# A transformer trunk on one core: first two projections interleaved, gate columns moved into the value weights, and the first query copies kept in the value tile

## The chip, the cores and the metric

The kernel runs on one core of a Trainium2 chip. The metric is the device time of one execution in microseconds (us). Three executions of the kernel before took 1258.33, 1259.99 and 1260.75 us.

## The reference

A trunk of two layers over 512 tokens of width 1024, with a memory of 256 rows that each layer attends to. Layer 0 mixes tokens by gated linear attention (GLA), layer 1 by a sparse attention (NSA); each layer ends in an FFN with a short convolution. The change touches layer 0 up to its memory attention:

```
xn = rmsnorm(h, norm_mix[i])
mem_kv = rmsnorm(mem, norm_mem[i]) @ w_mem_kv[i]
q, k, v, g, lr, mq = split_cols(xn @ gla_w_in[i], GLA_SIZES)   # 384, 384, 768, 768, 16, 256
log_a = log_sigmoid(lr @ gla_w_gate_up[i] + gla_b_gate[i]) / GLA_GATE_NORM
main = gla_mixer(q, k, v, log_a, g, gla_out_norm[i])
mo = mem_attention(mq, mem_kv)           # 4 heads of 64, softmax over 256 memory rows
h = h + concat([main, mo]) @ w_out[i]
h = h + conv_ffn(rmsnorm(h, norm_ffn[i]), ...)
```

## The kernel before, in words

Activations lie transposed: `h[k]` is a tile of 128 features by 512 tokens, k from 0 to 7. All large products run on TensorE (PE) as three fp32r matmuls on a split of each operand in a high part (`xh`, `wh`, a rounded copy made by ScalarE, ACT) and a low part (`xl`, `wl`, the remainder, made by VectorE, DVE): `xh·wh`, `xh·wl`, `xl·wh`. So one projection of 128 columns over 8 tiles of h is 24 matmuls of 512 columns (`projA`), and a projection whose result lies by tokens (`stepsB`, values) is, for each k and each of the four 128-token tiles, 3 matmuls. The rms norm's gain is folded into the split of h, and its row factor is applied later: `rms_sums` (sums of squares by 16 one-column matmuls, then the power on GpSimd, POOL) and `rms_rows` (four transposes, copied to `rb`).

Weights are packed in chunks of 128x1024 (512 KB). `wget` loads one by a DMA on SyncE's (SP's) queue into a `wraw` buffer (3 of them), and splits it into a `wh` and a `wl` buffer (3 each); so a split waits for the PE to be done with the chunk three before, and a load for the split of the chunk three before.

PSUM has four pairs of banks, `acc`, `sc`, `pt`, `po`. The framework orders the instructions of each engine by a planner with costs; `behind(a, b)` only forces a after b on an engine and adds no wait of its own.

The order of layer 0 before, on the PE: ten idle matmuls on ones; `glak[0]`, row by row as `h` comes in (L525), with the gate's small projection `lr` in three pieces between (L530: plain fp32, 16 output columns, summed from three places of a bank); `glaq[0]` and `glak[1]`, the latter with `rms_sums` and `rms_rows` in it; `glaq[1]`; the decays' up-projection `z` (L605) into two `po` and two `pt` banks, followed on ACT and DVE by Abs, Exp, Ln and a combining step (L606 to L611) that reads `z` again, and by the copies `lad` (`spread`, L615); `glak[2]` and `glaq[2]`; the memory's keys (`memk0`, two chunks, into `acc`) and values (`memv0`, into `po`); the memory queries (`glamq`, two chunks); then the memory attention, with the 768 value columns as filler between its steps (`fill`): 512 columns in four chunks, 256 in two.

For the memory attention the key and query halves of each head are stacked on 128 partitions: `dup` copies 64 rows twice by DMA (`kd` or `mt` from `mkf`, `qd` from `sq`), and the parts (`stack_k`, `stack_q`) are made from the copy. The keys' copies are issued by SP, those of the first queries by ACT's own queue. In the kernel before the query copies lie in tiles of the pool `mema0`.

Of the kernel before, what the change touches and what calls it, by code (L numbers as in the profile page):

```python
# [48 lines left out]
def pack_weights(i):  # L49
# [22 lines left out]
    moving("glav", gw, ar(1280, 1536), 4)  # L72
# [82 lines left out]
def host_inputs(i):  # L155
# [8 lines left out]
        "wlr": np.ascontiguousarray(_blocks(gw, np.arange(2304, 2320), 16)),  # L164
# [11 lines left out]
class Trunk:  # L176
# [29 lines left out]
    def setup(self):  # L206
        nc, I = self.nc, self.I
        self.wlr = self.const.tile([128, 152], F32, tag="wlr", name="wlr")[:, 24:]
        self.vec = self.t(self.const, [128, V_N], "vec")
        self.gains = self.t(self.const, [128, 64], "gains")  # L210
        self.h = [self.t(self.keep, [128, S], f"h{k}") for k in range(KC)]
        row = lambda eng, k: eng.dma_start(self.h[k], I["xT"][128 * k:128 * k + 128, :])
        self.raw = self.t(self.wraw, [128, 1024], "wraw")
        part = lambda c: nc.sync.dma_start(self.raw[:, 512 * c:512 * c + 512], I["wp"][self.W["glak"][0]][:, 512 * c:512 * c + 512])
# [12 lines left out]
        idle = self.ps("pt")  # L227
        for _ in range(10):
            nc.tensor.matmul(idle[:, :128], self.ones, self.ones, start=True, stop=True)
        self.mhalf = self.t(self.const, [128, 8], "mhalf")  # L230
        nc.scalar.activation(self.mhalf, self.ones[:, :8], AF.Copy, scale=-0.5)
# [5 lines left out]
    def gain(self, n, k):  # L237
        return self.gains[:, 8 * n + k:8 * n + k + 1]


    def wload(self, i):
        raw = self.t(self.wraw, [128, 1024], "wraw")
        self.nc.sync.dma_start(raw, self.I["wp"][i])
        return raw

    def wget(self, i, gain=None, ks=range(KC)):

        nc = self.nc
        raw = self.wload(i)
        wh = self.t(self.wsp, [128, 1024], "wh", FR)  # L250
        wl = self.t(self.wsp, [128, 1024], "wl", FR)
# [6 lines left out]
        if gain is not None:  # L258
            a, n = 8 * gain + ks[0], len(ks)
            g = self.gains[:, a:a + n].unsqueeze(2).to_broadcast([128, n, 1024 // n])  # L260
# [26 lines left out]
    def projA(self, ps, w, M=128, N=S, x=None, late=False, at=()):  # L287


# [6 lines left out]
        for n, (k, u, i) in enumerate(steps):  # L296
            if n in at:
                at[n]()
            self.last = self.nc.tensor.matmul(ps[:M, :N], u[:, M * k:M * k + M], x[k][i][:, :N], start=n == 0, stop=n == 23)  # L299

# [4 lines left out]
    def stepsB(self, name, first, rows, N, banks, x, gain=None):  # L305

        nc = self.nc
        for c in range(KC // rows):
            ks = range(rows * c, rows * c + rows)
            wh, wl = self.wget(self.W[name][first + c], gain, ks)  # L310
# [30 lines left out]
    def rms_sums(self, N, tag):  # L341
# [7 lines left out]
        self.powed = nc.gpsimd.tensor_tensor(out=self.rc, in0=self.rc, in1=self.mhalf[:, :nt], op=ALU.pow)  # L349

    def rms_rows(self, N, tag, after=None):

        pb = self.ps("pt")
# [23 lines left out]
    def stack_k(self, dst, kd):  # L377

        nc = self.nc
        nc.scalar.activation(dst, kd, AF.Copy)  # L380
        return nc.vector.tensor_tensor(out=dst[64:], in0=kd[64:], in1=dst[64:].bitcast(F32), op=ALU.subtract)

    def stack_q(self, qf, pool, qpool, bufs=1, eng=None):

        out = []
        for hh in range(2):
            qd = self.t(qpool, [128, S], "qd", bufs=2)
# [15 lines left out]
    def mem_kv(self, l, keep):  # L403
        nc, I = self.nc, self.I
        mK = []
        with self.tc.tile_pool(name=f"memp{l}", bufs=2, side="right") as pool:
# [10 lines left out]
            pk = [self.ps("acc") for _ in range(2)]  # L417
            self.projA(pk[0], self.wget(self.W[f"memk{l}"][0]), N=MEM, x=mx, at={12: lambda: self.rms_sums(MEM, "m")})
            self.projA(pk[1], self.wget(self.W[f"memk{l}"][1]), N=MEM, x=mx)
# [11 lines left out]
            for m in range(2):  # L431
                for hh in range(2):
# [3 lines left out]
                    self.stack_k(K, kd)  # L436
# [7 lines left out]
    def mem_att(self, qfs, pool, mK, mV, mo, first, fill, qpool, eng=None):  # L444
# [48 lines left out]
        Q[0] = self.stack_q(qfs[0], pool, qpool, eng=eng)  # L493
        first()
        for i in range(10):
            if i < 8:
                scores(*divmod(i, 4))
            if i == 3:
                Q[1] = self.stack_q(qfs[1], pool, qpool)
# [7 lines left out]
    def gla_layer(self):  # L507
        nc, I, tc = self.nc, self.I, self.tc
        with ExitStack() as outer:
# [8 lines left out]
            with tc.tile_pool(name="glap", bufs=1) as pp:  # L518
                wlr = self.wlr.rearrange("p (k c) -> p k c", k=8)
                nc.gpsimd.tensor_tensor(out=wlr, in0=wlr, in1=self.gains[:, :8].unsqueeze(2).to_broadcast([128, 8, 16]), op=ALU.mult)  # L520
                ps = self.ps("po")
                qps = [self.ps(tag) for tag in ("acc", "acc", "sc")]
                wh = self.t(self.wsp, [128, 1024], "wh", FR)
                wl = self.t(self.wsp, [128, 1024], "wl", FR)
                first = lambda u, k, i, **kw: nc.tensor.matmul(qps[0], u[:, 128 * k:128 * k + 128], self.x[k][i], **kw)  # L525

                def small(a, b, after):
                    for n in range(a, b):
                        o = 32 * ((n + 1) % 3)
                        gate = nc.tensor.matmul(ps[o:o + 16], wlr[:, n], self.h[n], start=n < 3, stop=n >= 5)  # L530
                        self.behind(gate, after)
                    return gate

                for k in range(KC):
                    self.split_x(0, [k])
                    if k < 2:
                        c = slice(512 * k, 512 * k + 512)
                        self.split_to(wh[:, c], wl[:, c], self.raw[:, c])
                    gate = small(0, 2, last) if k == 1 else None
                    for i in range(2):  # L540
                        last = first(wh, k, i, start=k + i == 0, stop=False)
                        if gate is not None:
                            self.behind(last, gate)
                    if k >= 2:
                        first(wl, k - 2, 0, start=False, stop=False)
                    if k == 4:
                        small(2, 5, last)
                for k in (KC - 2, KC - 1):
                    last = first(wl, k, 0, start=False, stop=k == KC - 1)
                small(5, 8, last)  # L550
                early = []
                for r, (name, j) in enumerate((("glaq", 0), ("glak", 1))):
                    for k in range(3 * r, 3 * r + 1 + 2 * r):
                        self.sq_step(k, self.h[k], S, after=self.made)
                    early.append(self.wget(self.W[name][j]))
                    if not r:
                        for k in (1, 2):
                            self.sq_step(k, self.h[k], S, after=self.made)
                nc.sync.dma_start(self.vec, I["vec"])
                for k in range(6, KC):  # L560
                    self.sq_step(k, self.h[k], S, after=self.made)

                def queries_keys(i):
# [3 lines left out]
                    else:  # L567
                        qp = self.ps("sc" if i == 3 else "acc")
                        self.projA(qp, self.wget(self.W[("glak", "glaq")[r]][j]))
                    sc = DK ** -0.5 if r else 1.0  # L570
                    for lo, hi, dst in ((0, DK, qk[:, :, r, j, :]), (DK, 128, qk[32 * j:32 * j + 32, :, r, 3, :])):
                        nc.vector.scalar_tensor_tensor(out=dst, in0=qp[lo:hi].rearrange("p (c t) -> p c t", c=4), scalar=sc,
                                                       in1=rb[lo:hi].rearrange("p (c t) -> p c t", c=4), op0=ALU.mult, op1=ALU.mult)

                for i in (1, 2):
                    self.projA(qps[i], early[i - 1], late=i == 1, at=self.rms_at(6, 18) if i == 2 else ())
                rc, rb = self.rc, self.rb
# [10 lines left out]
                lr = self.t(pp, [128, S], "lr")  # L588
                nc.gpsimd.memset(lr, 1.0)
                nc.scalar.copy(lr[:16], ps[:16])  # L590
                nc.vector.tensor_tensor(out=lr[:16], in0=ps[32:48], in1=lr[:16], op=ALU.add)
                nc.vector.tensor_tensor(out=lr[:16], in0=ps[64:80], in1=lr[:16], op=ALU.add)
                lrs = self.t(self.tmp, [128, S], "sq", FR, bufs=2)
                nc.vector.tensor_tensor(out=lr[:16], in0=lr[:16], in1=rb[:16], op=ALU.mult)
                nc.scalar.activation(lrs[:64], lr[:64], AF.Copy)
                nc.vector.tensor_tensor(out=lrs[64:], in0=lr[:64], in1=lrs[:64].bitcast(F32), op=ALU.subtract)
                for i in range(4):
                    queries_keys(i)
# [3 lines left out]
                for c in range(4):  # L602
                    z = self.ps("pt" if c >= 2 else "po")
                    for i, g in enumerate(gus):
                        nc.tensor.matmul(z[:, :384], lrs[:97, 128 * c:128 * c + 128], g, start=i == 0, stop=i == 1)  # L605
                    nc.scalar.activation(la[:, c, :], z[:, :384], AF.Abs)  # L606
                    pz.append(z)
                nc.scalar.activation(la, la, AF.Exp, scale=-1.0)
# [9 lines left out]
                for i in (4, 5):  # L618
                    queries_keys(i)
# [7 lines left out]
                with tc.tile_pool(name="memk0", bufs=1, side="right") as mk:  # L627
                    mK, mV = self.mem_kv(0, mk)
                    with tc.tile_pool(name="mema0", bufs=1, side="right") as mp:
# [3 lines left out]
                        for m in range(2):  # L633
                            qfs.append(self.project_q(w, rb, self.tmp, bufs=2, tag="sq"))
                            if m == 0:
                                w = self.wget(self.W["glamq"][1])

                        def values():
                            for g, (rows, N) in enumerate(((2, 512), (4, 256))):
# [883 lines left out]
```

## Time and profile before

| | |
|---|---|
| times of three runs | 1258.33, 1259.99, 1260.75 us; median 1259.99 |
| profiled execution | 1260.37 us, of which the span from first to last instruction is 1258.6 us |
| granted TensorE clock | 0.999 |
| PE, DVE, ACT, POOL busy | 1248.6, 816.4, 605.5, 119.0 us |
| chain that ended last | PE 91%, DMA 3%, DVE 3%, ACT 2% |

A row of the profile has the engine, the line of the kernel, the operation, the tile written and those read, shapes and a count. A matmul's own duration overlaps the next one; what a matmul costs in a stream is the distance from its start to the next start. In the timeline the bracket gives how long an engine was idle before the row and what released it.

### The profile page before, as it was taken

What the parts mean: (1) busy time and instruction counts of PE and PEld (TensorE: products, weight loads), DVE (VectorE), ACT (ScalarE), POOL (GpSimd) and SP (SyncE); (2) the same over time, 40 slices, a digit from 0 to 9 for tenths busy, and PEclk for the clock granted to TensorE, in tenths of its full rate; (3) what the DMA queues carried; (4) which work ended last, traced back from release to release, by engine and by line L of the source; (5) the groups of instructions that cost most, each with busy time, mean ns of one, the idle gap of its engine ahead of it and who ended that gap; (6) DMA issues with size and microseconds to landing.
All of it is one profiled execution on the core that took longest, in us unless ns stands there. A gap on an engine that the chain in (4) does not pass through costs nothing.

```text
span 1258.6 us, 18412 instructions
## 1 busy us (share of the span) xinstructions
PE 1248.6 (99%) x7054; PEld 1043.6 (83%) x7054; DVE 816.4 (65%) x1380; ACT 605.5 (48%) x1136; POOL 119.0 (9%) x144
## 2 busy tenths in 40 slices
PE   9999999999999999999999999999999999999998
PEld 6888889888888888888888788888888888888887
DVE  7756886577777774334677877855777777773331
ACT  7546654454444443223455677763544444442231
POOL 1000000000000000000102366650000000000000
PEclk9999999999999999999999999999999999999999
DMA  7651112343333333333766432303233333333321
GB/s 246 159 164 62 34 42 77 93 119 94 92 99 101 101 90 95 101 101 93 211 177 183 128 112 79 104 10 99 85 101 101 95 92 99 101 105 89 95 84 68
DMA packets 44891, 131.53 MB, mean 105 GB/s; under 512 B 6036, under 2 KB 11702, under 8 KB 44804
## 3 DMA queue, kind: packets, MB, share of 16 engines
q1 hardware_dynamic: 43124, 128.64, 35.3%
q10 hardware_dynamic: 1680, 1.72, 0.5%
q8 instruction: 56, 0.92, 0.3%
q14 instruction: 31, 0.25, 0.1%
HBM read 116.13 MB, written 2.15 MB: 94 GB/s over the span
## 4 chain that ended last, share of the span: by engine, by line
PE 91%; DMA 3%; DVE 3%; ACT 2%; issue 1%; SPq 0%; ACTq 0%; POOL 0%; POOLq 0%; DVEq 0%
PE acc L299 41%; PE acc L958 17%; PE acc L894 6%; PE po L1256 3%; PE acc L680 3%; PE acc L1256 3%; PE sc L1256 2%; PE pt L1257 2%; PE acc L1027 2%; PE acc L1170 2%; PE po L317 2%; PE sc L894 1%; DMA wraw<-in_wp 1%; PE pt L746 1%; PE acc L317 1%
## 5 line engine op out<-in xcount | busy, mean ns | idle before, releaser
L264 DVE TENSOR_TENSOR wl<-wraw,wh 128x1024 fp32r<-128x1024 f32 x180 | 229.3, 1274 | 139.8 <-ACT wh L263 137.3
L299 PE MATMUL acc<-xh,wh 128*128 128x512 f32 x792 | 308.9, 390 | 0.0
L299 PE MATMUL acc<-xl,wh 128*128 128x512 f32 x792 | 308.2, 389 | 0.0
L299 PE MATMUL acc<-xh,wl 128*128 128x512 f32 x792 | 307.0, 389 | 0.0
L263 ACT ACTIVATE wh<-wraw 128x1024 fp32r<-128x1024 f32 x180 | 190.8, 1060 | 226.7 <-PE acc L958 75.0
L299 PEld LDWEIGHTS acc<-xh,wh 128*128 128x128 f32 x792 | 148.7, 188 | 31.6 <-ACT sq L328 0.9
L299 PEld LDWEIGHTS acc<-xl,wh 128*128 128x128 f32 x792 | 148.7, 188 | 31.0
L299 PEld LDWEIGHTS acc<-xh,wl 128*128 128x128 f32 x792 | 148.7, 188 | 30.5
L958 PE MATMUL acc<-ah,wh 128*128 128x512 f32 x308 | 119.8, 389 | 0.0
L958 PE MATMUL acc<-ah,wl 128*128 128x512 f32 x308 | 119.8, 389 | 0.0
L958 PE MATMUL acc<-al,wh 128*128 128x512 f32 x308 | 119.8, 389 | 0.0
L939 DVE TENSOR_TENSOR u<-acc,rb 128x512 f32<-128x512 f32 x88 | 60.5, 688 | 73.7 <-PE acc L299 69.1
L277 ACT ACTIVATE ah<-hc 128x512 fp32r<-128x512 f32 x44 | 27.8, 632 | 117.1 <-DVE hc L946 117.1
L941 ACT ACTIVATE hc<-u,vec 128x512 f32<-128x512 f32 x88 | 71.1, 808 | 2.7 <-DVE u L939 2.0
L943 DVE SCALAR_TENSOR_TENSOR hc<-u,vec,hc 128x510 f32<-128x510 f32 x88 | 66.0, 750 | 3.0
L958 PEld LDWEIGHTS acc<-al,wh 128*128 128x128 f32 x308 | 57.8, 188 | 12.1
L945 ACT ACTIVATE hc<-hc 128x512 f32<-128x512 f32 x44 | 27.8, 632 | 83.1 <-DVE hc L943 83.0
L958 PEld LDWEIGHTS acc<-ah,wl 128*128 128x128 f32 x308 | 57.8, 188 | 12.0
L958 PEld LDWEIGHTS acc<-ah,wh 128*128 128x128 f32 x308 | 57.8, 188 | 11.9
L942 DVE SCALAR_TENSOR_TENSOR hc<-u,vec,hc 128x511 f32<-128x511 f32 x88 | 65.5, 744 | 1.8 <-ACT hc L941 1.8
L1335 POOL TENSOR_TENSOR P<-P,ssm 128x256 f32<-128x256 f32 (+3 forms) x48 | 63.3, 1339 | 1.8
L1327 ACT ACTIVATE P<-P,smn 128x128 f32<-128x128 f32 (+3 forms) x96 | 53.3, 558 | 6.6 <-DVE smn L1325 6.0
(407 smaller groups left out, 2107.4 us busy)
## 6 DMA issues: line engine op xcount, KB each, us to landing
wraw<-in_wp SPq DMA_DIRECT2D x197, 512.0 KB, 3.6
strip<-vecd SPq DMA_DIRECT2D x12, 448.0 KB, 4.1
qd<-qf SPq DMA_DIRECT2D x24, 128.0 KB, 2.4
h<-in_xT SPq DMA_DIRECT2D x8, 256.0 KB, 5.2
mt<-in_memT SPq DMA_DIRECT2D x16, 128.0 KB, 3.5
kd<-kf SPq DMA_DIRECT2D x16, 128.0 KB, 2.4
lad<-la SPq DMA_DIRECT2D x4, 384.0 KB, 7.5
qd<-sq SPq DMA_DIRECT2D x12, 128.0 KB, 2.8
```

Source lines behind the costliest of these rows:

```text
L263: self.made = nc.scalar.activation(wh, raw, AF.Copy)
L264: self.left = nc.vector.tensor_tensor(out=wl, in0=raw, in1=wh.bitcast(F32), op=ALU.subtract)
L299: self.last = self.nc.tensor.matmul(ps[:M, :N], u[:, M * k:M * k + M], x[k][i][:, :N], start=n == 0, stop=n == 23)
L894: self.nc.tensor.matmul(ps[:, cols], a[:, o], b[:, cols], start=start and i == 0 and k == ks[0], stop=stop and k == 5 and i == 2)
L939: nc.vector.tensor_tensor(out=u, in0=ps, in1=rb, op=ALU.mult)
L941: nc.scalar.activation(c, u, AF.Identity, scale=tap(2), bias=tap(3))
L942: nc.vector.scalar_tensor_tensor(out=c[:, 1:], in0=u[:, :S - 1], scalar=tap(1), in1=c[:, 1:], op0=ALU.mult, op1=ALU.add)
L943: nc.vector.scalar_tensor_tensor(out=c[:, 2:], in0=u[:, :S - 2], scalar=tap(0), in1=c[:, 2:], op0=ALU.mult, op1=ALU.add)
L958: nc.tensor.matmul(ps, a[:, o], x, start=n == 0, stop=n == 3 * NJ - 1)
L1256: mm = lambda *args, **kw: pe(nc.tensor.matmul(*args, **kw))
L1327: nc.scalar.activation(P[:, br, :n], P[:, br, :n], AF.Exp, scale=-1.0, bias=mn[:, br:br + 1], accum_out=f[:, j, br:br + 1])
L1335: nc.gpsimd.tensor_tensor(out=P, in0=P, in1=f[:, i, :].unsqueeze(2).to_broadcast([128, 2, 128 * t + 128]), op=ALU.mult)
```

## The change

- **Opening.** The first chunk of the queries is loaded beside that of the keys, both in halves between the rows of `h`, and `glak[0]` and `glaq[0]` run interleaved, in an order written out by hand (`begin`), with the splits on ACT and DVE chained in program order (`chained`). The row gains for the first norm come as an 8x128 tile `gT`, transposed on the PE behind the fifth of now nine idle matmuls; the load of the first 64 gain columns and the tile `gains` go, and later gains are read from `vec`.
- **Gate.** The gate's 16 columns are packed behind the last 256 value columns: `glavg`, four chunks of 128x544 used, 272 moving columns. This product now runs right after `glak[1]`, into banks `po`, `po`, `sc`, `pt`, with `rms_sums` and `rms_rows` in it; its gate columns are scaled (`lrT`), transposed back by four PE transposes during `glaq[1]` (`rows`), split, and the four decay products run between the matmuls of `glaq[1]` (`decay`, at steps 13, 16, 19, 22), the third into an `acc` bank.
- **Order.** `glak[2]` and `glaq[2]` move into the filler of the memory attention, in place of the 256 value columns; the memory's keys go to `sc` banks.
- **Query copies.** The copies `qd` lie in `v[:, t, :512]`, which the value product fills only later. ACT issues the copies of the first queries ahead of the last two memory keys' high parts, and DVE scales the first queries ahead of these keys' low parts.

```
-    moving("glav", gw, ar(1280, 1536), 4)
+    both = np.concatenate([ar(1280, 1536), ar(2304, 2320)])
+    a = _blocks(gw, both, 272).reshape(128, 4, 544)
...
 def setup(self):
         row(nc.sync, 0)
-        nc.scalar.dma_start(self.gains, I["vec"][:, :64])
-        nc.scalar.dma_start(self.wlr, I["wlr"])
-        part(0)
+        nc.scalar.dma_start(gT, I["gT"])
+        part(0, 0)
         row(nc.sync, 1)
-        part(1)
-        for k in range(2, KC):
+        part(1, 0)
+        row(nc.sync, 2)
+        row(nc.sync, 3)
+        part(0, 1)
+        row(nc.sync, 4)
+        part(1, 1)
+        for k in range(5, KC):
             row(nc.sync, k)
...
+        turned = nc.tensor.transpose(idle[:, 128:136], gT, self.ident[:8, :8])
+        self.behind(turned, last)
+        nc.vector.tensor_copy(self.first, idle[:, 128:136])
...
 def mem_kv(self, l, keep, banks="acc"):
+            w = self.wget(self.W[f"memk{l}"][1])
+            if l == 0:
+                self.behind(self.made, self.rowed)
...
+                    low = self.stack_k(K, kd)
+                    if m:
+                        self.later.append((self.made, low))
...
 def mem_att(...):
+        Q[0] = self.stack_q(qfs[0], pool, lambda hh: homes(0, hh), eng=eng)
+        if eng is not None:
+            for made, low in self.later:
+                self.behind(made, self.copied)
...
 def gla_layer(self):
+                row(0)
+                halfw(0, 0)
+                begin(A(H, 0), A(L, 0))
+                row(1)
+                begin(A(H, 1), A(Wl, 0), A(Wl, 1))
+                halfw(1, 0)
+                begin(B(H, 0), B(H, 1), A(L, 1), B(L, 0), B(L, 1))
+                row(2)
+                begin(A(H, 2), B(H, 2), B(Wl, 0), B(Wl, 1), A(Wl, 2), B(Wl, 2), A(L, 2), B(L, 2))
...
+                self.projA(qps[2], third, late=True)
...
+                pv = [self.ps(tag) for tag in ("po", "po", "sc", "pt")]
+                for n, _ in enumerate(self.stepsB("glavg", 0, 2, 272, pv, self.x)):
+                    if n == 4:
+                        bank = self.rms_sums(S, "")
+                    if n == 9:
+                        self.rms_rows(S, "", self.last, bank)
...
+                def rows():
+                    pb = self.ps("po")
+                    for t in range(4):
+                        self.behind(nc.tensor.transpose(pb[:16, 128 * t:128 * t + 128], lrT[:, t], self.ident), self.last)
+                    self.rowed = nc.scalar.activation(lrs[:16], pb[:16], AF.Copy)
...
+                at = {13 + 3 * c: lambda c=c: decay(c) for c in range(4)}
+                at[4] = rows
+                for _ in queries_keys(3, None, at):
+                    pass
...
-                    mK, mV = self.mem_kv(0, mk)
+                    mK, mV = self.mem_kv(0, mk, "sc")
...
+                                for made, low in self.later:
+                                    self.behind(low, self.evacuated)
...
+                            yield from self.stepsB("glav", 0, 2, 512, pv, self.x)
+                            for t in range(4):
+                                nc.scalar.activation(v[:, t, :512], pv[t], AF.Copy, scale=rc[:, t:t + 1])
+                            for i in (4, 5):
+                                yield from queries_keys(i)
...
-                            upto(6)()
+                            upto(6 if len(calls) < 5 else 9)()
-                        self.mem_att(qfs, mp, mK, mV, mo, upto(8), fill, mp, nc.scalar)
+                        self.mem_att(qfs, mp, mK, mV, mo, upto(8), fill, lambda m, hh: v[:, 2 * m + hh, :512], nc.scalar)
```

More of the change, by code (lines that the diff above doesn't have):

```diff
@@ L227, in setup @@
         idle = self.ps("pt")
-        for _ in range(10):
-            nc.tensor.matmul(idle[:, :128], self.ones, self.ones, start=True, stop=True)
+        warm = lambda: nc.tensor.matmul(idle[:, :128], self.ones, self.ones, start=True, stop=True)
+        for _ in range(5):
+            last = warm()
+        turned = nc.tensor.transpose(idle[:, 128:136], gT, self.ident[:8, :8])
+        self.behind(turned, last)
+        nc.vector.tensor_copy(self.first, idle[:, 128:136])
+        for _ in range(4):
+            self.behind(warm(), turned)
         self.mhalf = self.t(self.const, [128, 8], "mhalf")
@@ L309, in stepsB @@
             ks = range(rows * c, rows * c + rows)
-            wh, wl = self.wget(self.W[name][first + c], gain, ks)
+            wh, wl = self.wget(self.W[name][first + c], gain, ks, rows * N)
             for r, k in enumerate(ks):
@@ L527, in small @@
[L527 to L534, printed above, removed]
-                    self.split_x(0, [k])
[L536 to L558, printed above, removed]
+                ws = [[self.t(self.wsp, [128, 1024], tag, FR) for tag in ("wh", "wl")] for _ in range(2)]
@@ new lines, in gla_layer, with chained, row, halfw @@
+                first = []
+                splits = []
+                def chained():
+                    for ins, n in ((self.made, 0), (self.left, 1)):
+                        if splits:
+                            self.behind(ins, splits[0][n])
+                    splits[:] = [(self.made, self.left)]
+                def row(k):
+                    self.split_x(0, [k])
+                    chained()
+                def halfw(n, c):
+                    c = slice(512 * c, 512 * c + 512)
+                    self.split_to(ws[n][0][:, c], ws[n][1][:, c], self.raw[n][:, c])
+                    chained()
@@ new lines, in begin @@
+                def begin(*parts):
+                    for n, u, i, k in parts:
+                        ins = nc.tensor.matmul(qps[n], ws[n][u][:, 128 * k:128 * k + 128], self.x[k][i], start=k + u + i == 0, stop=k == KC - 1 and i == 1)
+                        if first:
+                            self.behind(ins, first[0])
+                        first[:] = [ins]
+                H, L, Wl = (0, 0), (0, 1), (1, 0)
+                A, B = ((lambda p, k, n=n: (n, *p, k)) for n in range(2))
+                row(0)
@@ L559, in gla_layer @@
+                begin(A(H, 4), A(Wl, 4))
+                halfw(1, 1)
+                begin(B(H, 4), A(L, 4), B(L, 4), B(Wl, 4))
+                for k in range(5, KC):
+                    row(k)
+                    begin(*(t(p, k) for p in (H, Wl, L) for t in (A, B)))
+                self.sq_step(0, self.h[0], S, after=self.made)
+                third = self.wget(self.W["glak"][1])
                 nc.sync.dma_start(self.vec, I["vec"])
-                for k in range(6, KC):
+                for k in range(1, KC):
@@ L567, in queries_keys @@
                     else:
-                        qp = self.ps("sc" if i == 3 else "acc")
-                        self.projA(qp, self.wget(self.W[("glak", "glaq")[r]][j]))
+                        qp = self.ps("acc")
+                        yield from self.stepsA(qp, self.wget(self.W[("glak", "glaq")[r]][j]), at=steps)
                     sc = DK ** -0.5 if r else 1.0
                     for lo, hi, dst in ((0, DK, qk[:, :, r, j, :]), (DK, 128, qk[32 * j:32 * j + 32, :, r, 3, :])):
[L572 to L577, printed above, removed]
+                        ins = nc.vector.scalar_tensor_tensor(out=dst, in0=qp[lo:hi].rearrange("p (c t) -> p c t", c=4), scalar=sc,
+                                                             in1=rb[lo:hi].rearrange("p (c t) -> p c t", c=4), op0=ALU.mult, op1=ALU.mult)
+                        if after is not None:
+                            self.behind(ins, after)
+                self.projA(qps[2], third, late=True)
                 gup = self.t(pp, [128, 384], "gup")
```

120 lines of the change are left out of this document (63 added, 57 removed).

## The prediction

> **What bounds the kernel now.** I read the page first, then the PE's timeline up to 120 us, then ACT, DVE and SP around the places where the PE waits.
>
> ```profile
> PE 1248.6 (99%) x7054; PEld 1043.6 (83%) x7054; DVE 816.4 (65%) x1380; ACT 605.5 (48%) x1136; POOL 119.0 (9%) x144
> ```
>
> The PE is the bound: of the span's 1258.6 us only 10 have no matmul running. A busy PE need not be at its pace, so the pace is taken from start to start. In these rows of the PE's timeline the reader is to look at the first column; between the pairs lie 14, 34 and 4 intervals:
>
> ```profile
> 16.47 0.39 PE L299 MATMUL acc<-xl,wh 128*128 128x512 f32 x1
> 19.66 0.39 PE L299 MATMUL acc<-xl,wh 128*128 128x512 f32 x1
> 48.42 0.28 PE L299 MATMUL acc<-mh,wl 128*128 128x256 f32 x1
> 52.50 0.28 PE L299 MATMUL acc<-ml,wh 128*128 128x256 f32 x1
> 34.06 0.86 PE L605 MATMUL po<-wg,sq 97*128 97x384 f32 x4
> 34.76 0.85 PE L605 MATMUL pt<-wg,sq 97*128 97x384 f32 x4
> ```
>
> 512 columns take 3.19/14 = 0.2275 us, 256 take 4.08/34 = 0.12, 384 take 0.70/4 = 0.175. One column more costs (0.2275 - 0.12)/256 = 0.42 ns. Held against these paces, the starts up to 120 us show time lost in only three places, all touched by the change: the opening with the gate's pieces, the norm sums, and the first scores of the memory attention.
>
> **The opening, term a.** First two windows (busy time by engine; last the clock, DMA share and GB/s), then what ACT, DVE and the PE did:
>
> ```profile
> 2.00:12.00 10.00, 8.59 (x41) 5.26 (x39) 6.27 (x10) 8.00 (x13) 0.40 (x1) 1.00 1.00 362
> 5.83:21.70 15.87, 15.15 (x64) 9.04 (x65) 14.11 (x19) 13.85 (x22) 1.85 (x3) 1.00 0.93 321
> 3.85 0.72 ACT L280 ACTIVATE xh<-h,gains 128x512 fp32r<-128x512 f32 x1 [0.69 <-DMA gains<-in_vec]
> 5.14 0.63 ACT L277 ACTIVATE wh<-wraw 128x512 fp32r<-128x512 f32 x1 [0.57 <-DMA wraw<-in_wp]
> 7.17 0.63 ACT L277 ACTIVATE wh<-wraw 128x512 fp32r<-128x512 f32 x1 [0.58 <-DMA wraw<-in_wp]
> 8.61 4.13 DVE L281 SCALAR_TENSOR_TENSOR xl<-h,gains,xh 128x512 fp32r<-128x512 f32 x6
> 5.83 0.50 PE L525 MATMUL acc<-xh,wh 128*128 128x512 f32 x1 [0.69 <-ACT wh L277]
> 15.16 1.04 PE L530 MATMUL po<-h,wlr 128*16 128x512 f32 x6
> 16.13 0.50 PE L299 MATMUL acc<-xh,wh 128*128 128x512 f32 x1
> ```
>
> From 5.83 to 21.70, where the third projection starts, 64 matmuls run: 48 of two projections, worth 48 x 0.2275 = 10.92, and the gate's 16. A piece of six holds the PE for 16.13 - 15.16 = 0.97. The rest of the 15.87 is waiting for rows.
>
> After, the 16 go, and 48 matmuls have two weight halves to work on. The first needs the gain, row 0 and the first half. `gT` is an eighth of the bytes of the load it replaces, and waits for five idle matmuls; the half landed at 5.14 and keeps its place in the queue, so I leave the first matmul at 5.8. Then five matmuls can run (to 6.95) until the first half of the queries, which takes the queue place of the half that landed at 7.17, is split on ACT by 7.8. That is a stall of 0.9; 43 matmuls are left, and end at 7.8 + 43 x 0.2275 = 17.6. Is the rest in time? Twelve pieces of 0.262 MB are 3.15 MB; at 362 GB/s from 2.0 they drain by 10.7, and a piece lands up to 2 later (the one of 7.17 ends 1.15 MB into the queue, drained by 5.2 at this rate), so row 7 is there by 12.7. ACT has 8 x 0.72 + 4 x 0.63 = 8.3 us of splits from 3.9, with waits for two landings: done near 13.5. DVE has 4.13/6 = 0.69 to 0.75 a row and 0.69 a half: done near 14.3. The PE comes to row 7 at 16.2. So the third projection starts at 17.6 in place of 21.70: **a = -4.1**. With the stall gone and a start at 5.6 it is -4.7; with rows 0.9 later than the PE wants them -3.2.
>
> **Sums, columns and transposes, terms b, c, d.**
>
> ```profile
> 23.52 0.39 PE L299 MATMUL sc<-xl,wh 128*128 128x512 f32 x1
> 24.06 0.63 PE L338 MATMUL pt<-ones,sqacc 128*64 128x1 f32 x16 [0.15 <-DVE sqacc L332]
> 24.62 0.50 PE L299 MATMUL sc<-xh,wh 128*128 128x512 f32 x1
> 26.80 0.60 PE L355 MATMUL pt<-ident,rc 128*128 128x128 f32 x4
> 27.15 0.48 PE L299 MATMUL sc<-xh,wh 128*128 128x512 f32 x1
> ```
>
> The sums waited 24.06 - 23.75 = 0.3 for DVE. In the value product they come at 17.6 + 5.46 + 12 x 0.127 = 24.6, while the squares' adds can start near 15: **b = -0.3** (0 if DVE is late again). The four row transposes, 27.15 - 26.80 = 0.35, only move.
>
> The value product has 96 matmuls of 272 instead of 256 columns: 96 x 16 x 0.42 ns, **c = +0.65**; it costs 12.2 at its new place, and the keys and queries 4 and 5 give 10.9 of filler where it gave 11.5. Four chunks instead of two are 2 more splits; DVE, which was busy 14 of the opening's 16 us, is freed of the gate's adds, and the PE has three chunks ahead, so I cost them at nothing; if that cover were gone, a chunk's two splits, some 1.3 by the whole chunk's 2.3, would show.
>
> Four new transposes bring `lrT` back: **d = +0.35**, by the rows just used. They are pinned behind matmul 4 of `glaq[1]`, so every later matmul waits with them for DVE's four small scalings and for a `po` bank; the first decay is pinned 9 matmuls (2.0 us) behind, with ACT's copy and a DVE subtraction between. If DVE has one chunk's split in front, d is 1.3. The decay matmuls cost 8 x 0.175 as before.
>
> **The first queries' copies, term e.** Three views: ACT, DVE and the PE around the first scores; and the landing times of the tile `qd`.
>
> ```profile
> 64.04 0.39 PE L299 MATMUL acc<-xh,wh 128*128 128x512 f32 x1
> 64.96 0.42 ACT L380 ACTIVATE mK<-mkd 128x256 fp32r<-128x256 f32 x1 [2.27 <-DMA mkd<-mkf]
> 65.87 0.69 DVE L400 SCALAR_TENSOR_TENSOR sq<-acc,rb 128x512 f32<-128x512 f32 x1
> 66.65 2.47 ACTq L375 DMA_DIRECT2D qd<-sq  x4
> 73.22 0.63 ACT L277 ACTIVATE Qh<-qd 128x512 fp32r<-128x512 f32 x1 [6.07 <-DMA qd<-sq]
> 75.21 0.28 PE L454 MATMUL sc<-mK,Ql 128*128 128x256 f32 x1
> 75.99 0.39 PE L454 MATMUL sc<-mK,Qh 128*128 128x256 f32 x1 [0.50 <-ACT Qh L277]
> 76.72 0.39 PE L454 MATMUL sc<-mK,Ql 128*128 128x256 f32 x1 [0.34 <-DVE Ql L278]
> DMA to landing us min/median/max: 2.3/4.9/6.1
> ```
>
> The scores lose 75.99 - 75.33 and 76.72 - 76.11, 1.27 in all. The cause lies ten microseconds earlier: the scaling of the queries (65.87) stands on DVE behind the last key's low part, which needs the key's copy (64.96), while the first queries' product was through at 64.04, where the second one's stream begins. The change lifts the scaling to about 64.2 and the issue to 65.0, 1.7 earlier. The keys moved behind are needed only four scores later, some 20 us on: nothing for them. Landing then decides. The copies took up to 6.1 us, the first pair from 66.65 to 73.22; after the change the decays' copies (next) come nearer too. **e = -1.0**, between -1.27 and 0.
>
> [...]
>
> **The decays' chain, term f.** ACT, DVE, SP and the PE in order of time, a window, and from the page the splits of a weight chunk on DVE and ACT (mean ns of one behind the comma):
>
> ```profile
> 37.11 1.47 ACT L608 ACTIVATE la<-la 128x1536 f32<-128x1536 f32 x1
> 38.60 1.28 ACT L609 ACT_TABLE_LOAD   x1
> 39.89 1.58 ACT L609 ACTIVATE la<-la,ones 128x1536 f32<-128x1536 f32 x1
> 41.51 1.02 DVE L611 SCALAR_TENSOR_TENSOR la<-po,la 128x384 f32<-128x384 f32 x2 [1.76 <-ACT la L609]
> 43.52 1.37 SPq L615 DMA_DIRECT2D lad<-la  x2
> 46.35 0.28 PE L299 MATMUL acc<-mh,wh 128*128 128x256 f32 x1
> 52.62 0.28 PE L317 MATMUL po<-wh,mh 128*128 128x256 f32 x1
> 45.00:58.00 13.00, 13.00 (x109) 12.62 (x108) 8.36 (x13) 3.47 (x4) 0.70 (x1) 1.00 1.02 233
> L264 DVE TENSOR_TENSOR wl<-wraw,wh 128x1024 fp32r<-128x1024 f32 x180 | 229.3, 1274 | 139.8 <-ACT wh L263 137.3
> L263 ACT ACTIVATE wh<-wraw 128x1024 fp32r<-128x1024 f32 x180 | 190.8, 1060 | 226.7 <-PE acc L958 75.0
> ```
>
> The memory values (52.62) take the two `po` banks that hold `z` until DVE's last step (41.51). That left 10 us; the change takes nearly all of it. By my walk: third projection 17.6 to 23.1, value product with sums and rows to 36.2, `glaq[1]` with 0.35 and 1.4 to 43.4, memory keys 6.27 (52.62 - 46.35) to 49.7. The last decay ends near 43.0; Abs 0.4, Exp 1.47, table 1.28, Ln 1.58, two steps of 0.51 bring the `po` banks free at 48.8. Slack 0.9. But ACT and DVE must also split the memory values' first chunk (1.06 and 1.27), whose buffer comes free at 43.4: ahead of Exp it delays the banks to 49.9, behind Ln it comes itself at 51. **f = +0.4**, between 0 and 1.4. The copies `lad` move from 43.5 to 50 on SP, and with them the stretch from 45 to 58, in which DMA was full (share 1.02): up to the keys' copies, and towards those of the queries. Their own reader comes only in the filler, over 20 us on.
>
> **Sum.** -4.1 - 0.3 + 0.65 + 0.35 - 1.0 + 0.4 = **-4.0**. The profiled execution took 1260.37, its span 1258.6 and 1.8 around it; so 1256.4 for it, and against the median 1259.99, 0.4 lower, **1256.0**. Ends: -4.7 - 0.3 + 0.65 + 0.3 - 1.27 = -5.3, 1254.7; -3.2 + 0.65 + 1.3 + 1.4 = +0.15, 1260.1.
>
> **The rivals.**
> *The earlier copies land no earlier* (e = 0). For it: DMA was full where they now go, and the decays' copies follow close. Against: 1.7 us is more than the 1.27 lost. -3.0: 1257.0.
> *The memory stage gives it back.* The PE comes 3 us sooner to banks, chunks and copies that come later: f 1.4, d 1.3, e 0. For it: a slack under 1 us where 10 were. Against: ACT was busy only 3.47 of the 13 us from 45 on. -4.1 - 0.3 + 0.65 + 1.3 + 1.4 = -1.05: 1258.9. No change, by the bound of a measurement of this kernel, 0.2% or 2.5 us.
> *Slower: the decays' chain holds the `po` banks.* One mechanism: ACT serves memory rows and weight chunks ahead of Abs, Exp and Ln, and the PE stands before the memory values. Without f the sum is -4.4; it decides from a stall of 6.9 on, the banks free at 56.6 instead of 48.8. At a stall of 8: 1263.6. For it: eight memory rows of squares and splits and three chunks of 1.06 could stand in front. Against: these rows ran before 43 in the kernel before, and ACT is freer before that now.
>
> **How the numbers follow.** Forecast 0.48; copies no earlier 0.19; given back 0.17; slower 0.10; better than every term (1254.7 and less) 0.06. The second lies within half a microsecond of the bound at 1257.5: I give 0.11 of it to faster. Faster 0.48 + 0.11 + 0.06 = 0.65, same 0.08 + 0.17 = 0.25, slower 0.10. Range 1254.0 to 1259.6: out are the slower case and half of the best. The forecast's own is 1254.7 to 1257.3.
>
> **What would show it.** a: the first L299 matmul of `glak[1]` near 17.6, no gap above 1 us after 5.8. b: no wait before the 16 one-column matmuls. c: starts 0.127 apart in the value product. d: matmuls 4 and 13 of `glaq[1]` without a wait. e: the copies issued less than 1 us after the first query product ends, the scores without a wait. f: the first memory value matmul directly behind the keys. The prediction is wrong if row 7 lands after 14, if the PE waits over 1.5 us ahead of the memory values, or if the scores still wait 1.3.

## The result and the profile after

| | before | after |
|---|---|---|
| median (lowest to highest), us | 1259.44 (1258.33 to 1260.75) | 1272.50 (1270.68 to 1273.30) |
| ratio after to before | | 1.0101, 95% interval 1.0085 to 1.0117 |
| profiled execution, span | 1260.37, 1258.6 | 1270.68, 1268.9 |
| first GLA chunk's first matmul | 116.02 | 126.29 |

The change made the kernel slower by 13 us by the medians, where I had forecast 4 us faster. The last row of the table, from the PE's timelines of both kernels, shows where to look: of the 10.3 us between the two profiled executions, all are lost before 126 us, and behind that both run at one pace. The profiled execution of the change is the shortest of its four; what the longer three lost besides stands in no trace.

```profile
116.02 0.69 PE L711 MATMUL sc<-lev,la 128*96 128x512 f32 x2
```

```profile
126.29 0.70 PE L785 MATMUL sc<-lev,la 128*96 128x512 f32 x2
```

The opening does what was said: the third projection starts at 17.35 (21.70 before). Then the gain goes in two stands of the PE. The first, in ACT, DVE, POOL and PE rows of the kernel after, put in order of time:

```profile
29.87 0.42 ACT L349 ACTIVATE sqm<-mt 128x256 f32<-128x256 f32 x1 [2.94 <-DMA mt<-in_memT]
30.32 0.42 DVE L353 TENSOR_TENSOR sqaccm<-sqaccm,sqm 128x256 f32<-128x256 f32 x1 [1.85 <-ACT sqm L349]
30.66 0.15 DVE L369 TENSOR_SCALAR rc<-pt 128x4 f32<-128x4 f32 x1
30.99 1.11 POOL L370 TENSOR_TENSOR rc<-rc,mhalf 128x4 f32<-128x4 f32 x1 [11.96 <-DVE rc L369]
32.16 0.65 PE L377 MATMUL pt<-ident,rc 128*128 128x128 f32 x4 [3.65 <-POOL rc L370]
48.35 0.28 PE L319 MATMUL sc<-mh,wh 128*128 128x256 f32 x1
54.60 0.35 PE L338 MATMUL po<-wh,mh 128*128 128x256 f32 x1
```

The sums of the norm (L359) are done by 26.4, but the mean (L369), a DVE step of 0.15 us, comes at 30.66. It stands in DVE's order behind the add of a memory row's squares (L353), that waits for ACT's square (L349), and that for the memory row's load. So the PE stands 3.65 us ahead of the norms' row transposes, and the memory keys start at 48.35 instead of 46.35. The memory values follow the keys at once (54.60): the decays' chain holds no bank.

The second stand is longer. ACT, then the PE, then DVE:

```profile
67.11 4.27 ACTq L397 DMA_DIRECT2D v<-sq  x4
71.42 0.42 ACT L402 ACTIVATE mK<-mt 128x256 fp32r<-128x256 f32 x1 [6.84 <-issue]
75.34 0.63 ACT L294 ACTIVATE Qh<-v 128x512 fp32r<-128x512 f32 x1 [3.20 <-DMA v<-sq]
78.55 0.63 ACT L294 ACTIVATE Qh<-v 128x512 fp32r<-128x512 f32 x1 [2.58 <-DMA v<-sq]
79.09 2.94 ACT L280 ACTIVATE wh<-wraw 128x1024 fp32r<-128x1024 f32 x3
76.03 0.80 PE L482 MATMUL sc<-mK,Qh 128*128 128x256 f32 x2 [4.24 <-ACT Qh L294]
79.23 0.58 PE L482 MATMUL sc<-mK,Qh 128*128 128x256 f32 x1 [1.90 <-ACT Qh L294]
80.18 1.22 PE L338 MATMUL acc<-wh,xh 128*128 128x512 f32 x2
66.39 0.69 DVE L422 SCALAR_TENSOR_TENSOR sq<-acc,rb 128x512 f32<-128x512 f32 x1 [1.35 <-PE acc L319]
```

The first queries are scaled right behind their product (66.39) and their copies issued at once, as predicted. But the issue of four copies takes ACT 4.27 us (2.47 before), they land near 75.3 and 78.5, and ACT's work behind the issue is late: the keys' high parts directly, the value weights' splits because they stand behind the high part of the second copy (78.55). The PE has no values to run meanwhile: their first weights are split only from 79.09. SP's queue shows why:

```profile
55.97 1.36 SPq L687 DMA_DIRECT2D lad<-la  x2
58.54 5.38 SPq L397 DMA_DIRECT2D mt<-mkf  x6
63.95 1.23 SPq L397 DMA_DIRECT2D mkd<-mkf  x2
65.23 1.28 SPq L687 DMA_DIRECT2D lad<-la  x2
66.61 4.06 SPq L260 DMA_DIRECT2D wraw<-in_wp  x3
```

The decays' copies `lad` went out between 43.5 and 50.2 before; now two go at 55.97 and two at 65.23, right where the keys' copies, the queries' copies and the value weights' loads are, and the value weights' loads come last (66.61). Before, the first of these was out by 53.4, ahead of the keys' copies (the second of the two from 50.32).

Windows of the kernel after (busy us by engine, then granted clock, DMA share, GB/s) show a third loss:

```profile
72.00:74.00 2.00, 0.00 (x0) 0.00 (x0) 1.32 (x3) 0.14 (x1) 0.00 (x0) 1.00 1.06 300
76.00:84.00 8.00, 6.08 (x16) 4.65 (x17) 4.11 (x5) 5.42 (x8) 0.00 (x0) 0.50 0.59 148
86.00:90.00 4.00, 4.00 (x20) 3.30 (x19) 1.81 (x8) 1.06 (x1) 0.00 (x0) 1.00 0.78 249
```

After 4.24 us of standing, the granted clock is 0.50, and the matmuls from 80.18 to 84.96 run at half rate: those of 512 columns start 0.43 us apart, where the pace before was 0.2275.

The account up to the first GLA chunk, by starts against the paces of the prediction: +2.1 when the first query product starts (60.72 against 58.58); 4.40 + 0.48 + 2.36 + 0.26 + 0.24 = 7.7 of standing around the first scores, where 1.27 was lost before; 2.2 at half rate; -0.6 for the filler, as predicted. That is 2.1 + 6.4 + 2.2 - 0.6 = 10.1, of the 10.27 seen.

### The profile page after: what moved, and what is told of

Read it like the earlier page. It is cut to its first block, busy times and chain, and to the rows that moved or that the text cites. A ratio compares the mean times of both kernels' runs of the same rounds, so it can differ in the third digit from the quotient of the medians.

```text
span 1268.9 us, 18395 instructions
## 1 busy us (share of the span) xinstructions
PE 1250.4 (99%) x7041; PEld 1047.1 (83%) x7041; DVE 814.2 (64%) x1385; ACT 606.6 (48%) x1138; POOL 118.2 (9%) x144
## 4 chain that ended last, share of the span: by engine, by line
PE 95%; DMA 2%; issue 1%; DVE 0%; ACTq 0%; ACT 0%; POOL 0%; SPq 0%; POOLq 0%; DVEq 0%
PE acc L319 43%; PE acc L1032 17%; PE acc L968 6%; PE po L1330 3%; PE po L338 3%; PE acc L754 3%; PE acc L1330 3%; PE acc L338 2%; PE sc L1330 2%; PE pt L1331 2%; PE acc L1101 2%; PE acc L1244 2%; PE sc L968 1%; PE pt L820 1%; DMA mt<-in_memT 1%
## 5 line engine op out<-in xcount | busy, mean ns | idle before, releaser
L281 DVE TENSOR_TENSOR wl<-wraw,wh 128x1024 fp32r<-128x1024 f32 (+1 forms) x181 | 229.4, 1268 | 138.2 <-ACT wh L280 135.7
L280 ACT ACTIVATE wh<-wraw 128x1024 fp32r<-128x1024 f32 (+1 forms) x181 | 189.9, 1051 | 222.9 <-PE acc L1032 75.0
```

Of the source, the lines that this page charges most:

```text
L280: self.made = nc.scalar.activation(wh, raw, AF.Copy)
L281: self.left = nc.vector.tensor_tensor(out=wl, in0=raw, in1=wh.bitcast(F32), op=ALU.subtract)
```

## The experiments

The theory from these readings: the decays' copies, moved later, fall into the query copies and the value weights' loads. Rivals: the copies' new place and the orderings beside them; the norm wait; the lowered clock. The edits are shown shortened; comments in them stand for what is left out.

**The decays' copies behind the value weights' loads.** Both `spread` calls go into the second call of `fill` and are held behind the third value chunk's load on SP; the first two are out by 59.5 here.

```
-                spread(0)
-                        spread(1)
+                            if len(calls) == 2:      # in fill
+                                spread(0); spread(1) # each behind(self.loaded)
```

> The changed kernel, with the four copies of the decays issued on SP behind the third value chunk's load, where before they were issued as soon as the decays were ready. Theory A (queue order): in the changed kernel the first value chunk's load was issued at 66.6 us, behind the decays' copies and the keys' copies, so the PE had no filler when it waited for the scores, stood for 4.2 and 1.9 us, and ran at half clock after that. Then here the load goes ahead of the keys' copies, the PE finds value matmuls directly behind the second query product (71.6 us), the stall of 71.6 to 80 goes, and the time falls by 7 to 9, to 1263 to 1265. Theory B (the query copies in their new place, issued ahead of the last keys, land late): the scores still come near 76 to 79; only what the filler covers is won, and the time stays above 1268.

Measured: 1267.89 us, ratio 1.0072 (1.0057 to 1.0087). About a third of the loss is gone; the time lies between what the two theories gave. The values now run ahead of the scores, but the PE stands again (ACT, then the PE):

```profile
68.07 6.93 ACTq L397 DMA_DIRECT2D v<-sq  x4
75.04 0.42 ACT L402 ACTIVATE mK<-mt 128x256 fp32r<-128x256 f32 x1 [6.64 <-issue]
77.03 0.79 PE L338 MATMUL acc<-wh,xh 128*128 128x512 f32 x1 [3.38 <-DVE sq L422]
```

With all four `lad` copies in flight (issued 66.18 to 72.15), the issue on ACT takes 6.93. The last keys' parts are ordered behind it, the second queries' scaling behind these, and the values wait for its `acc` bank.

**The mean ahead of the memory rows.** DVE's adds and low parts of memory rows from the sixth on stand behind the mean.

```
+                if l == 0 and k >= 5:
+                    self.behind(self.added, self.meaned)
+                    self.behind(self.left, self.meaned)
```

> The changed kernel, with DVE's adds and low parts of the last three memory rows forced behind the norm's mean. Theory C (in-order DVE): the wait of 3.65 us before the row transposes came from the mean standing on DVE behind an add that waited for a memory row's transfer. Then the wait falls under 0.5 and everything up to the second query product comes 3.3 us earlier. If what follows is bound by work that moves with it, the time falls by 3 to 3.5, to about 1269; if the stall at the scores hangs on transfers that do not move, it grows by as much and the time stays at 1272.

Measured: 1270.71 us, ratio 1.0094 (1.0079 to 1.0109). The wait at the row transposes falls from 3.65 to 1.28, not under 0.5, and a wait of 0.95 comes up at the decays' row transposes:

```profile
29.89 0.32 PE L377 MATMUL pt<-ident,rc 128*128 128x128 f32 x1 [1.28 <-POOL rc L370]
```

The memory keys start at 47.53 instead of 48.35, but the second stand swallows most of it: the scores wait for the queries' copies and start at 75.2 and 79.1, against 76.0 and 79.2. (From here on, kernels that name the mean have line numbers 3 higher.)

**The copies in their own tiles, the orderings gone.**

```
-            for made, low in self.later: self.behind(made, self.copied)
-                                for made, low in self.later: self.behind(low, self.evacuated)
-  ... lambda m, hh: v[:, 2 * m + hh, :512], nc.scalar)
+  ... lambda m, hh: self.t(mp, [128, S], "qd", bufs=2), nc.scalar)
```

> The changed kernel without its last part: the query copies lie in tiles of their own again, and no key part is ordered behind them or the scaling. Theory B (the copies' new place and order cause the stall): the time falls to 1264 to 1266. Theory A (queue order): the first value chunk's load stays behind the decays' and keys' copies, so the stall stays; the scaling of the first queries stands behind the last keys again and the copies come 2 to 4 us later: 1272 to 1276.

Measured: 1271.46 us, ratio 1.0101 (1.0086 to 1.0116): the same as the change. The copies' new place and the orderings are not what makes the change slow; the PE stands 5.49 us ahead of the first scores here too. The copies' place alone, with the orderings kept, was not tried: copies into the keys' old space would wait for key parts that are ordered behind them.

**Nine idle matmuls behind the second query product.**

```
+                        for _ in range(9):
+                            self.behind(nc.tensor.matmul(idle[:, :128], self.ones, self.ones, start=True, stop=True), self.last)
```

> The changed kernel with nine idle matmuls of 128 columns behind the second query product, in the stall. Theory D (clock): the profile's windows of the changed kernel show a granted clock of 0.65 to 0.50 from 74 to 84 us and 512-column matmuls 0.425 apart instead of 0.2275; with the idle work the clock stays at 1.00 in the stretch, the 13 or so matmuls and scores at half pace win 2 to 3 us, and the time falls to 1269 to 1270. If the clock costs nothing that the stall would not cost anyway, because the scores wait for copies in that time, the time stays within 1 us of 1272. The planner sets the order of the first scores a little differently here.

Measured: 1273.59 us, ratio 1.0120 (1.0103 to 1.0137). No gain: they end at 75, the PE then stands till 82.48, and the clock falls as before. The planner also put the first values ahead of the scores here, so only the run with 96 below is compared with this one.

**Decays' copies as in the first experiment, query copies as in the third.** The decays' copies stand behind the third value chunk's load here too (issued from 66.54 on).

```
+                            if len(calls) == 2: spread(0); spread(1)   # behind(self.loaded)
-            for made, low in self.later: self.behind(made, self.copied)
+  ... lambda m, hh: self.t(mp, [128, S], "qd", bufs=2), nc.scalar)
```

> The decays' copies (L687) stand behind the first value weights' load, as in the run with the late decays' copies (1267.9 us), and in addition the first queries' copies go into tiles of their own and the orderings that put the second key tile's parts behind these copies are gone. If the ordering is what turned the slow copies into the 3.5 us stand of the PE for an `acc` bank (73.3 to 77.0), the key parts run ahead of the copies, the second query's scaling follows its product at once, the values follow without a gap over 1 us, and the time is 1262 to 1264. If the full DMA engines are the cause, the four copies still take 5 to 7 us to issue on ACT, whatever stands behind them waits as before, and the time is 1266 to 1268.

Measured: 1269.71 us, ratio 1.0081 (1.0065 to 1.0098). That is slower than either theory gave. The theory of the ordering falls. The key parts run ahead now and the `acc` bank comes in time, but the issue on ACT takes as long, and the scores wait instead (ACT and PE):

```profile
69.06 6.93 ACTq L397 DMA_DIRECT2D qd<-sq  x4
77.86 0.63 ACT L294 ACTIVATE Qh<-qd 128x512 fp32r<-128x512 f32 x1 [8.80 <-DMA qd<-sq]
83.36 0.58 PE L482 MATMUL sc<-mK,Qh 128*128 128x256 f32 x1 [3.70 <-ACT Qh L294]
```

**The decays' copies behind all query copies.** The orderings are back; `spread` moves to the fifth call of `fill`, behind the second pair of query copies.

```
-                            if len(calls) > 3:
+                            if len(calls) > 6:
                                 next(lds, None)
+                            if len(calls) == 5:
+                                spread(0); spread(1)  # each behind(self.copied)
```

> All four decays' copies (L687) are issued after the second pair of query copies, and their parts for the chunks two calls later; everything else is as in the changed kernel, the orderings included. Theory of the traffic: the first queries' copies meet only weight loads, their issue on ACT takes 2.5 to 3.5 us, as in the kernel before (2.47), not 4.27 or 6.93, the key parts start by 71.5, the PE has no gap over 1.5 us between the second query product and the scores and is never at half clock there, and the time is 1262 to 1264, the opening's 3.7 us wait for the norms being still there. Theory of the ordering: ACT's issue of the copies stays ahead of the key parts and the PE still stands 2 us or more for the `acc` bank: 1266 to 1268.

Measured: 1261.57 us, ratio 1.0017 (1.0008 to 1.0026): 11 us less than the change. The theory of the traffic holds (ACT, then SP):

```profile
67.95 2.50 ACTq L397 DMA_DIRECT2D v<-sq  x4
70.50 0.42 ACT L402 ACTIVATE mK<-mt 128x256 fp32r<-128x256 f32 x1 [2.21 <-DVE wl L281]
72.46 0.63 ACT L294 ACTIVATE Qh<-v 128x512 fp32r<-128x512 f32 x1 [1.23 <-DMA v<-sq]
75.82 5.14 SPq L687 DMA_DIRECT2D lad<-la  x4
```

No stand is left around the scores, and the first GLA chunk comes at 117.15. What remains is the norm wait, with a lowered clock behind it (PE row and window row of this kernel):

```profile
31.51 1.12 PE L377 MATMUL pt<-ident,rc 128*128 128x128 f32 x4 [3.46 <-POOL rc L370]
32.00:34.00 2.00, 2.00 (x10) 2.00 (x10) 1.80 (x4) 0.93 (x2) 0.00 (x0) 0.50 0.25 33
```

**The opening's waits taken away as well.**

```
+                if l == 0 and k >= 3:                 # adds and low parts behind the mean
-                    if n == 9:
+                    if n == 11:                       # rms_rows
-                at = {13 + 3 * c: ...}; at[4] = rows
+                at = {16 + 2 * c: ...}; at[8] = rows
```

> As the run with all decays' copies after the query copies, and in addition the opening's waits are taken away: the DVE's work on the memory rows from the fourth row on stands behind the mean of the norms, the norms' row transposes stand two value steps later, and the decays' row transposes four matmuls later in the fourth projection. If these waits (3.7 us before the norms' transposes; 1.1 us at the decays' transposes in the run with the mean first) lie on the path, the memory keys start 3 to 4.5 us earlier than in the run beside it (near 44.5) and the time is 2 to 4 us under it, 1258 to 1261. If a later transfer sets the end (the keys' copies or the weights' loads, which the DMA engines deliver at their own pace), the earlier start is lost before the GLA chunks and the two runs agree within 1 us.

Measured: 1257.05 us, ratio 0.9982 (0.9972 to 0.9991), the fastest kernel of the study: 4.5 us under the run beside it, more than expected, and 1.9 under the kernel before. The waits lay on the path, and what ran at half rate behind the first of them too: from the row transposes to the memory keys the run beside it took 17.67 us (31.51 to 49.18), the kernel after, whose clock stayed up there, 16.19. So 3.46 of wait and about 1.5 of half rate could be won, and the memory keys start 4.47 earlier here. PE rows:

```profile
28.86 0.60 PE L377 MATMUL pt<-ident,rc 128*128 128x128 f32 x4
44.71 0.28 PE L319 MATMUL sc<-mh,wh 128*128 128x256 f32 x1
73.61 0.28 PE L485 MATMUL sc<-mK,Qh 128*128 128x256 f32 x1
112.64 0.70 PE L788 MATMUL sc<-lev,la 128*96 128x512 f32 x2
```

No bracket in front of the row transposes and the scores: nothing waits. The first GLA chunk is 3.4 us earlier than before (112.64 against 116.02).

**Only the place of the first value weights' load.** The keys' copies stand behind it on SP.

```
+            if name == "glav" and c == 0:
+                for ins in self.keycopies:
+                    self.behind(ins, self.loaded)
```

> Only the place of the first value weights' load on SP is changed: ahead of the keys' copies instead of behind them and behind the decays' copies. If the place of this load makes the PE idle after the second query product (values only at 80.2), the values start before the scores at about 72, the half clock does not come, and the time is 1264 to 1267, that is 4 to 8 us under the changed kernel. If the traffic and the slow issue of the copies are the cause, the values are early but the PE then stands for the `acc` bank or the scores as in the run with the late decays' copies, and no more than 3 us are gained: 1268 to 1270.

Measured: 1265.54 us, ratio 1.0046 (1.0031 to 1.0061), 7 us under the change, as the theory of the load's place has it: two stands remain, the clock stays at 1.00 there.

```profile
73.99 0.50 PE L342 MATMUL acc<-wh,xh 128*128 128x512 f32 x1 [0.61 <-ACT wh L281]
76.39 0.51 PE L489 MATMUL sc<-mK,Qh 128*128 128x256 f32 x2 [1.21 <-ACT Qh L295]
```

It does not part the two causes, though. The decays' copies lay ahead of the load and so went out together at 57.56, before the query copies (68.70). What parts them is the pair of the first experiment and the run with the decays' copies behind all query copies. Both have the first two value weights' loads out by 59.5, the query copies in the value tile and the orderings; only the decays' copies, and with them the making of their parts, are placed otherwise. 6.3 us lie between them, and the eight query copies into the value tile take 8.3 us in the median (4.5 to 10.4) to land in the first, 3.7 (2.2 to 4.8) in the second. How much of the 13 us is the load's place and how much the traffic, no run tells by itself.

**The copies' place again, without stands.** The kernel of 1257.05 us with the first query copies in tiles of their own and no orderings.

```
-  ... lambda m, hh: v[:, 2 * m + hh, :512], nc.scalar)      # and the two loops over self.later
+  ... lambda m, hh: self.t(mp, [128, S], "qd", bufs=2), nc.scalar)
```

> As the run with the opening's waits taken away and the decays' copies after the query copies (1257.05 us, ratio 0.9982), but the first queries' copies lie in two tiles of their own again and the second key tile's parts are ordered behind nothing, as in the kernel before. The order of the PE's instructions is the same in both. If the copies' place in the value tile is worth what the prediction gave it (1.0 us, the second copy not waiting for the reader of the key copies), the scores wait here and the time is 1258.0. If the copies' place only moves transfers that the values cover, the times agree: 1257.0, with no wait over 0.3 us at the first scores in either trace.

Measured: 1257.85 us, ratio 0.9994 (0.9986 to 1.0003). The medians lie 0.8 apart, but the intervals of the ratios overlap. The first scores wait in neither trace; this one's first GLA chunk is 0.6 later, which lies at the fourth projection's first low weights (a wait of 0.76 at 37.92), not at the copies. I take the place and the orderings as worth nothing here that can be measured.

```profile
74.21 0.28 PE L485 MATMUL sc<-mK,Qh 128*128 128x256 f32 x1
```

**The clock by itself.** 96 idle matmuls where the fourth experiment had nine.

```
-                        for _ in range(9):
+                        for _ in range(96):
```

> The changed kernel with 96 idle 128-column matmuls instead of nine behind the second query product (at about 0.1 us each they last some 9.6 us, as long as the PE stood there in the run with nine, 72.9 to 82.5). With nine the granted clock fell to 0.50 by 80 and the time was 1273.59. If standing idle is what lowers the clock and the half rate costs time behind the stand, the granted clock stays at 1.00 through 90, the value matmuls behind it run at 0.23 us and not 0.43, and the time is 1.5 to 3 us under that of the run with nine, 1270.5 to 1272. If the clock follows the time of the records or the load of the DMA engines and not the PE's standing, it falls here too and the times agree.

Measured: 1283.80 us, ratio 1.0200 (1.0185 to 1.0216). The time expected was missed since I had the idle matmuls too cheap: from the first of them to the values behind them it took 21.35 us (72.76 to 94.11), 0.22 each, not 9.6 in all. The run with nine had shown as much, 2.2 us for nine. The question is answered all the same. The first value matmul and a window of the run with nine, then the same and two windows of this one:

```profile
82.48 1.22 PE L338 MATMUL acc<-wh,xh 128*128 128x512 f32 x2 [7.43 <-ACT wh L280]
80.00:82.00 2.00, 0.00 (x0) 0.00 (x0) 0.49 (x1) 1.15 (x2) 0.00 (x0) 0.50 0.28 65
```

```profile
94.11 0.48 PE L338 MATMUL acc<-wh,xh 128*128 128x512 f32 x1
78.00:80.00 2.00, 2.00 (x20) 2.00 (x19) 0.00 (x0) 0.00 (x0) 0.00 (x0) 1.00 1.06 287
94.00:98.00 4.00, 4.00 (x21) 3.36 (x20) 0.00 (x0) 0.00 (x0) 0.00 (x0) 1.00 0.00 0
```

While the PE works the clock stays at 1.00 in both windows, in the first with a DMA share of 1.06. The values start 11.6 us later (94.11 against 82.48), the first GLA chunk 9.95 later (138.79 against 128.84). So the half rate cost about 1.7 us, if the somewhat other order of the first scores costs nothing.

## Why the prediction was wrong

**a, the opening, held:** -4.35 against -4.1 forecast. **c** held: the value product's starts lie 0.127 apart. **d** held: the decays' row transposes wait for nothing in the kernel after. **f** was 0, at the low end of 0 to 1.4, and with it the slower rival falls: the `po` banks came in time.

**b failed.** The sums wait no more, but I wrote that the row transposes "only move". They moved to a place where DVE's order puts the mean behind work on memory rows whose loads land at the same time. I had looked at what the sums wait for, not at what the mean stands behind: the 0.3 was won, and a stand of 3.65 came in its place.

**e failed, and decided the sign.** I forecast -1.0 and bounded it by 0 on the bad side. The steps up to the issue were right. The landing was taken from the kernel before as 2.3 to 6.1 us. That view mixed the copies of two queues: the four that ACT issued took 5.9 to 6.1, and the shorter times, 2.3 to 4.9, are those of later copies on SP. I left it at that, though I had written under f that the copies `lad` move "towards those of the queries". With them in flight the issue on ACT took 4.27 us and the copies 7.6 in the median to land (6.0 before), and the PE lost 7.7 around the first scores instead of 1.27: +6.4 where I had -1.0. I had no reason that excluded a loss, and should have taken a bound above nothing: copies some 3 us later, with the scores and the value weights' splits both behind them.

**Two things stood in no term.** The value weights' load lost its place on SP, because the memory values' splits came later and the decays' and keys' copies went first; I had costed the weight chunks at nothing without following their loads through the queue. And I counted a stand as its length only; behind it 2.2 us went at half rate. The clock fell at the row transposes as well: of the eight profiles with a stand of 3.46 to 3.78 us before them, seven show a granted clock of 0.50 to 0.54 in the lowest window behind it; in that of the change itself (3.65) it stayed at 1.00, as it did behind the 1.28 of the run with the mean first. What sets the 3.65 apart was not shown. Whether the longer executions of the change lost time in that way was not shown.

The first rival, with e = 0, pointed the right way, but counted only the landing. The issue took time of its own: 1.07 us a copy on average in the kernel after, beside 7.6 to landing, and four in a row held ACT for 4.27, and the keys' high parts with it.

In the kernel of 1257.05 us, with both faults mended, the first GLA chunk comes 3.4 us earlier by the traces, against 4.0 forecast. The value product took 0.6 more (13.7 us, forecast 13.1) and the fourth projection 0.65 more (7.85 against 7.2); f gave back its 0.4, and e came to the full -1.27. By the medians the gain is only 1.9; the profiled execution of before, 1260.37, is one of its longer ones (1257.85 to 1261.33 on the chip of that comparison).

## What to carry to other kernels

When a chain of work moves later, its DMAs move too: list what else lands in the new stretch and whose issue, on which engine, stands among them. Before a short step is called free, look at what stands in front of it in its engine's order, and whether that waits for a transfer: a mean of 0.15 us stood here behind an add that started at 30.32. And look at the clock behind a stand of the PE: it was 0.50 to 0.54 in seven of the eight profiles that had one of 3.46 to 3.78 us before the row transposes.

## What I had not expected of the hardware

ACT's issue of the same four copies of 128 KB took 4.27 us in one kernel, 6.93 and 2.53 in others. Windows over the issue in the kernel after, the first experiment, and the kernel of 1257.05 us:

```profile
67.11:71.38 4.27, 4.27 (x20) 3.55 (x19) 0.00 (x0) 0.00 (x0) 0.00 (x0) 1.00 0.97 161
```

```profile
68.07:75.00 6.93, 5.58 (x25) 4.30 (x23) 1.23 (x1) 0.34 (x1) 0.00 (x0) 1.00 1.05 208
```

```profile
63.48:66.01 2.53, 2.53 (x13) 2.10 (x12) 1.23 (x1) 0.34 (x1) 0.00 (x0) 1.00 1.00 342
```

The DMA share is 0.97 to 1.05 in all three, so the share does not tell the fast issue from the slow ones: 2.53 us at 342 GB/s, 4.27 and 6.93 with the decays' copies under way, at 161 and 208 GB/s. Why fewer bytes move there at the same share, and what in the decays' copies goes with the slow issue, was not tried and stays open.
